# Encoder layer on one core: Squares one row tile ahead, the second w_ada group between the blocks, the fifth pair's weight parts behind the sums

## The chip, the core and the metric

The kernel runs on one NeuronCore of one Trainium2 chip, as one launch. Its engines work side by side: TensorE (PE) multiplies matrices into PSUM banks, VectorE (DVE) and ScalarE (ACT) work elementwise and empty the banks, GpSimd (POOL) sets buffers and issues some stores, and SyncE (SP) issues nearly all transfers. Each engine takes its own instructions strictly in their order and waits on semaphores for the others. The metric is the device time of one execution in microseconds; smaller is better.

## What is computed

The reference is one layer of an encoder on x (1024 rows of 2048), with the parameters of a vector c:

```python
mod = jax.nn.silu(c) @ w_ada + b_ada
shift, scale, gate = jnp.split(mod, 3, axis=-1)
h = rmsnorm(x, pre_g) * (1.0 + scale[:, None]) + shift[:, None]
proj = h @ w_in
...
y_a = windowed_gqa(q, k, v, rel_table, sink) * jax.nn.silu(gate_a)
y_p = multiscale_pool(u, w_pool_grp, pool_scale) * jax.nn.silu(gate_p)
g = jax.nn.sigmoid(h @ w_merge + b_merge)
merged = g_a * (y_a @ w_br_attn) + g_p * (y_p @ w_br_pool)
o = merged @ w_out
return x + gate[:, None] * rmsnorm(o, post_g)
```

All of it is float32. The change touches the first hundred microseconds alone: the norm of x, shift and scale, the making of h, and the first products with w_in.

## The kernel before

**Products.** Every float32 operand is split into a high and a low part (`split`: ACT copies the high part, DVE subtracts it for the low part), and a product is three passes: high by high, high by low, low by high. The large products run by a Strassen scheme (`strassen`): for a pair of 128-column blocks of weights, seven products (X, V and Z are their PSUM banks) with seven moving operands, made from the four quarters of h transposed and named in `MOVING`: B11, T3, T2, B21, T4, T1, B22. "h" and "l" behind a name are the high and low part; whi and wlo are the parts of the weights, raw their loaded tile, ws a sum of two of its quarters.

**The ramp.** x has eight row tiles of 128 rows: 0 to 3 are the left half of h transposed (first index 1 or B11, B21), 4 to 7 the right half (B12, B22). h transposed has 16 tiles k of 128 features; j counts pairs of them. A row tile is normed by `norm_rows` (Squares on ACT and DVE with sums, a DVE reduce of the four sums, then a Sqrt on ACT) and scaled by `scale_rows` on DVE; `turn_part` transposes it on PE (XT) into a PSUM bank, and `take_turned` copies the bank out. A feature tile then needs its scale and shift: `modulation(j)` multiplies silu(c) by 16 tiles of w_ada in four steps (GEMV), ACT copies the sums (acc), PE transposes them (PM), and DVE makes modc of them. Group j = 0 serves k = 0 and 1, group j = 1 k = 2 and 3.

Only then can operands be made. The first four pairs of weight columns (`AHEAD_PAIRS`) take their share of k = 0 and 1 as plain blocks, without the scheme: `plain_blocks(i, s)` is pair i with the left (s = 0) or right (s = 1) half, two PSUM banks of six matmuls (PB), which ACT copies out (c) and POOL's queue stores. `fill_half` makes the operands of these blocks, `fill_sums(0)` those sums of k = 0 and 1 that only the scheme needs, `fill(1)` all operands of k = 2 and 3. With both, pairs five to eight run through the scheme (`ramp_gen`); the first of them, the fifth pair, starts with X at B11.

**What sets the order.** The instructions are put on each engine by a scheduler, but those given to `keep` stay in the order of the program text. The blocks, transposes, GEMVs, Squares, scaling and sums are all kept, so the text from `g0 = modulation(0, ...)` to `fill(1)` sets PE's order, and ACT's and DVE's for the kept ones. `warm(n)` puts n matmuls without a use (WARM) between others. `OPEN` matmuls write the two banks "z0" and "z1" once before Z uses them; they can do so only after ACT has copied the last transposes out of the same banks. `early` and `held` are pools of buffers that end where they are closed.

In the program before, the text is: three steps of group 0 with WARMs, its sums, `fill_half(0)`, `norm_rows(4)`, then for each of four pairs `scale_rows`, `plain_blocks(m, 0)` and the next `norm_rows`; the transposes of k = 0 and 1 with seven WARMs between; `fill_half(1)`; the four pairs' right halves with transposes of k = 2 to 7 between them, and group 1's four steps spread over the last two of them, its PM behind the last block.

Of the kernel before, what the change touches and what calls it, by code (L numbers as in the profile page):

```python
# [43 lines left out]
def encoder_layer(ctx: ExitStack, tc: tile.TileContext, x, c, table, w_ada, b_ada, pre_g,  # L44
# [46 lines left out]
    def keep(ins):  # L91

        tc.keep_in_program_order(ins)

# [9 lines left out]
    @contextmanager  # L104
    def behind(name):

        if name in anchor:
            with tc.issue_after(anchor[name].ins):
                yield
        else:  # L110
            yield
# [110 lines left out]

    def strassen(w, n0, rows, js, op, ev, finish, part=None, raws=None, given=()):

# [45 lines left out]
        def first_weights():  # L270
            yield from given
            if not given:
                yield prep(a11)
                s3 = wp.tile([P, nj, P], F32, tag="ws", name=uid("ws"))
                sub(s3, a11, a21)
                yield prep(s3)
            with behind("blocks" if given else None):
                add(a21, a21, a22)
                sub(a11, a21, a11)
            yield prep(a11)  # L280
# [317 lines left out]
    def fill_sums(j):  # L598

        (b11, b12), (b21, b22) = ((xT[k, 0], xT[k, 1]) for k in (2 * j, 2 * j + 1))  # L600
        keep(sub(b12, b12, b11))
        t2 = rp.tile([P, 512], F32, tag="tf", name=uid("tf"), bufs=2)
        keep(sub(t2, b22, b12))
        keep(sub(b11, t2, b11))
        split(*op["T3"][j], b11, True)
        split(*op["T2"][j], t2, True)
        keep(sub(b21, b21, t2))
        for name, src in (("T4", b21), ("T1", b12)):
            split(*op[name][j], src, True)
# [4 lines left out]
    def ramp_gen(js, i, parts, last):  # L614
        w, n0 = weight_of(RAMP_ORDER[i])
        dst = block(part_d, RAMP_ORDER[i]) if last else block(ramp_d[i], 0)
        return strassen(w, n0, rows_in_turn(0), js, op, ev, to_dram(dst), parts, raws.pop(0))

# [97 lines left out]
    g0 = modulation(0, ada[0].__getitem__, True, True)  # L716
    for step in g0[:2]:
        step()
        warm(3)
    g0[2]()  # L720
    warm(4)
    g0[3]()
    g0[4]()
    warm(3)
    fill_half(0)
    ssq = norm_rows(4)
    for m in range(4):
# [24 lines left out]
    s0, s1, s2, s3, _ = modulation(1, ada[1].__getitem__, True)  # L752
    s0()
    s1()
    plain_blocks(2, 1)
    turn_next((6, 7))
    s2()
    for tag in SEEDED:
        hi = op["B11"][0][0]
        keep(nc.tensor.matmul(bank(tag, "OPEN"), hi[:, 0:P], hi, start=True, stop=True))  # L760
    s3(lambda: plain_blocks(3, 1))
    held.close()
# [924 lines left out]
```

## Time and profile before

| | |
|---|---|
| median of 3 runs | 2110.8 us (2109.87 to 2112.79) |
| the profiled execution | 2110.36 us, its span 2108.6 us |
| mean granted TensorE clock in it | 0.996 |
| PE, DVE, ACT busy | 2074.4, 1549.4, 1112.1 us |

The span is the time from the first to the last instruction of one execution that the hardware profiler recorded; 1.8 us of that execution lie around it. A row of the timeline gives start and duration in us, engine, source line, operation, output<-input by the program's names, shapes and the number of merged instructions; the brackets hold the engine's idle time before it and what ended that. A row of windows gives for a stretch the busy time of each engine with its number of instructions, then the clock that PE was granted (1.00 is full), the DMA engines' busy share (over 1 means more than one transfer at once on an engine) and GB/s.

### The profile page before, as it was taken

How to read it: one execution, taken by the hardware profiler on the slowest of the kernel's cores; microseconds unless marked ns; L12 is line 12 of the kernel's file. 1: busy time of each engine (PE TensorE's matmuls, PEld its weight loads, DVE VectorE, ACT ScalarE, POOL GpSimd, SP SyncE). 2: the span in 40 equal slices, each digit the busy share in tenths (PEclk: the TensorE clock that was granted, in tenths of full speed). 3: DMA queues.
4: the chain of work that ended last, by engine and by line, in shares of the span. 5: the costliest groups of instructions: out<-in, count | busy, mean ns of one | idle time of the engine just before them, and what ended most of it. 6: DMA issues, size and time to landing. Idle time of an engine off the chain costs nothing.

```text
span 2108.6 us, 28906 instructions
## 1 busy us (share of the span) xinstructions
PE 2074.4 (98%) x9473; PEld 1704.8 (81%) x9473; DVE 1549.4 (73%) x2787; ACT 1112.1 (53%) x2114; POOL 42.2 (2%) x135
## 2 busy tenths in 40 slices
PE   6999999999999999999999999999999999999998
PEld 3678788788888888888888888888888788888886
DVE  5696678788547776677777678857957977889667
ACT  5663344444574544665666544333645645767554
POOL 1100000000000000000000000010000000000000
PEclk9999999999999999999999999999999999999999
DMA  9966778999676355454545476675745556686897
GB/s 329 333 216 226 256 246 287 311 320 300 207 242 207 129 176 196 165 166 161 197 153 166 150 241 228 216 239 180 249 156 172 178 195 200 223 308 203 297 332 248
DMA packets 304171, 474.49 MB, mean 225 GB/s; under 512 B 24323, under 2 KB 144235, under 8 KB 304020
## 3 DMA queue, kind: packets, MB, share of 16 engines
q1 hardware_dynamic: 297664, 455.70, 65.3%
q0 software_dynamic: 4896, 14.73, 1.8%
q10 hardware_dynamic: 1460, 2.22, 0.3%
q8 instruction: 74, 1.21, 0.2%
q14 instruction: 77, 0.63, 0.1%
HBM read 344.60 MB, written 130.05 MB: 225 GB/s over the span
## 4 chain that ended last, share of the span: by engine, by line
PE 95%; DVE 2%; DMA 2%; ACT 0%; issue 0%; DVEq 0%; ACTq 0%
PE Z L248 31%; PE X L248 21%; PE V L248 21%; PE Z L1394 2%; PE Z L1396 2%; PE Z L1395 2%; PE X L1395 1%; PE V L1396 1%; PE V L1395 1%; PE X L1396 1%; PE V L1394 1%; PE X L1394 1%; PE PB L691 1%; DMA xt<-in_x_dram 1%; PE PT L1104 1%; PE GEMV L494 1%
## 5 line engine op out<-in xcount | busy, mean ns | idle before, releaser
L96 ACT ACTIVATE whi<-raw 128x512 fp32r<-128x512 f32 (+2 forms) x528 | 319.5, 606 | 527.2 <-PE Z L248 253.3
L97 DVE TENSOR_TENSOR wlo<-raw,whi 128x512 fp32r<-128x512 f32 (+2 forms) x528 | 344.2, 656 | 153.9 <-PE Z L248 121.7
L97 DVE TENSOR_TENSOR wlo<-wr,whi 128x512 fp32r<-128x512 f32 x224 | 150.4, 689 | 51.5 <-ACT whi L96 48.3
L96 ACT ACTIVATE whi<-wr 128x512 fp32r<-128x512 f32 x224 | 138.2, 629 | 87.5 <-DVE wlo L97 30.5
L114 DVE TENSOR_TENSOR raw<-raw,raw 128x512 f32<-128x512 f32 (+1 forms) x80 | 54.7, 683 | 86.0 <-DMA raw<-in_w_merge_dram 57.4
L248 PE MATMUL V<-T3h,whi 128*128 128x512 f32 x332 | 91.1, 393 | 2.3 <-ACT whi L96 1.3
L248 PE MATMUL X<-B11h,whi 128*128 128x512 f32 x332 | 90.8, 391 | 2.3 <-ACT B11h L96 2.3
L248 PE MATMUL Z<-T2h,wlo 128*128 128x512 f32 x332 | 90.2, 391 | 0.8 <-DVE wlo L97 0.8
L96 ACT ACTIVATE whi<-ws 128x512 fp32r<-128x512 f32 (+2 forms) x88 | 53.5, 608 | 71.1 <-PE X L248 62.4
L248 PE MATMUL X<-B11l,whi 128*128 128x512 f32 x332 | 90.2, 390 | 0.8 <-DVE B11l L97 0.8
L114 DVE TENSOR_TENSOR u<-V,u 128x512 f32<-128x512 f32 x94 | 64.6, 687 | 35.6 <-PE V L248 35.0
L248 PE MATMUL X<-B21h,whi 128*128 128x512 f32 x332 | 90.6, 392 | 0.0
L248 PE MATMUL Z<-B22h,whi 128*128 128x512 f32 x332 | 90.6, 392 | 0.0
L248 PE MATMUL Z<-T2h,whi 128*128 128x512 f32 x332 | 90.4, 392 | 0.1
L248 PE MATMUL V<-T3l,whi 128*128 128x512 f32 x332 | 90.4, 391 | 0.0
L248 PE MATMUL Z<-T1h,whi 128*128 128x512 f32 x332 | 90.4, 390 | 0.0
L248 PE MATMUL Z<-T2l,whi 128*128 128x512 f32 x332 | 90.3, 391 | 0.0
L248 PE MATMUL V<-T3h,wlo 128*128 128x512 f32 x332 | 90.1, 391 | 0.0
L248 PE MATMUL V<-T4h,whi 128*128 128x512 f32 x332 | 90.1, 391 | 0.0
L248 PE MATMUL X<-B21l,whi 128*128 128x512 f32 x332 | 89.8, 390 | 0.0
L248 PE MATMUL Z<-B22l,whi 128*128 128x512 f32 x332 | 89.8, 390 | 0.0
L248 PE MATMUL Z<-T1l,whi 128*128 128x512 f32 x332 | 89.8, 389 | 0.0
(366 smaller groups left out, 4882.9 us busy)
## 6 DMA issues: line engine op xcount, KB each, us to landing
part<-part_d SPq DMA_DIRECT2D x136, 256.0 KB, 4.9
ada<-in_w_ada_dram SPq DMA_DIRECT2D x128, 256.0 KB, 6.0
raw<-in_w_merge_dram SPq DMA_DIRECT2D x64, 512.0 KB, 5.7
wr<-ws_dS SPq DMA_DIRECT2D x60, 512.0 KB, 5.3
raw<-in_w_in_dram SPq DMA_DIRECT2D x56, 512.0 KB, 4.0
wr<-in_w_out_dram SPq DMA_DIRECT2D x48, 512.0 KB, 5.3
proj_d<-part SPq DMA_DIRECT2D x68, 256.0 KB, 2.2
sw<-in_w_out_dram SPq DMA_DIRECT2D x64, 256.0 KB, 5.2
```

Of the source, the lines that this page charges most:

```text
L96: ins = (nc.scalar.activation(hi, src, AF.Copy), nc.vector.tensor_tensor(lo, src, f32(hi), ALU.subtract))
L97: nc.vector.tensor_tensor(lo, src, f32(hi), ALU.subtract))
L114: return (eng or nc.vector).tensor_tensor(o, a, b, ALU.add)
L248: nc.tensor.matmul(ps, w_[:, i], op[mov][j][m_], start=fresh and i == 0 and n == 0, stop=i == nj - 1 and n == 2, skip_group_check=True)
L494: ins = nc.tensor.matmul(pv[g:g + 32, :], scz[:, kc, :], tile_of(kc), start=kc < 4, stop=kc >= 12, tile_position=(0, g))
L691: keep(nc.tensor.matmul(open_[nt], w[:, kh, nt * P:(nt + 1) * P], mov[kh][m], start=n == 0, stop=n == 5, skip_group_check=True))
L1104: nc.tensor.transpose(pt[:, i * P:(i + 1) * P], p[:, i * P:(i + 1) * P], ident)
L1394: nc.tensor.matmul(pb, hi, w[0], start=first, stop=False, skip_group_check=True)
L1395: nc.tensor.matmul(pb, lo, w[0], start=False, stop=False, skip_group_check=True)
L1396: nc.tensor.matmul(pb, hi, w[1], start=False, stop=last, skip_group_check=True)
```

## The change

Three things move, and no product is added or dropped.

1. `norm_rows(4)` is issued before the last step of group 0, and inside the loop each `norm_rows` stands ahead of the `scale_rows` of the row tile before it. The WARMs are set anew: five after each of three steps and five after the sums (20 for 13), none between the transposes of k = 0 and 1 (0 for 7), two before the second column's blocks.
2. Group 1's steps are issued after the first right-half pair and its transposes (two steps) and after the second (two steps), with the transposes of k = 4 and 5 between the copy acc and PM. The last two pairs' right halves follow.
3. `strassen` gets `hold`: for the fifth pair, the preparation of its first weight parts (whi, wlo, the sums ws) is issued behind the last split of `fill_sums(0)`, on ACT and on DVE (`anchor["sums", ...]`). Before, `given` and the anchor "blocks" were there without a use.

```diff
-    def behind(name):
+    def behind(name, engine):
-        if name in anchor:
-            with tc.issue_after(anchor[name].ins):
+        if (name, engine) in anchor:
+            with tc.issue_after(anchor[name, engine].ins):
...
         def first_weights():
-            yield from given
-            if not given:
-                yield prep(a11)
-                s3 = wp.tile([P, nj, P], F32, tag="ws", name=uid("ws"))
+            with behind(hold, "v"), behind(hold, "a"):
+                w = prep(a11)
+            yield w
+            s3 = wp.tile([P, nj, P], F32, tag="ws", name=uid("ws"))
+            with behind(hold, "v"), behind(hold, "a"):
                 sub(s3, a11, a21)
-                yield prep(s3)
-            with behind("blocks" if given else None):
+                w = prep(s3)
+            yield w
+            with behind(hold, "v"):
                 add(a21, a21, a22)
                 sub(a11, a21, a11)
...
         for name, src in (("T4", b21), ("T1", b12)):
-            split(*op[name][j], src, True)
+            hi, lo = op[name][j]
+            anchor["sums", "a"] = keep(nc.scalar.activation(hi, src, AF.Copy))
+            anchor["sums", "v"] = keep(sub(lo, src, f32(hi)))
...
-    for step in g0[:2]:
+    for step in g0[:3]:
         step()
-        warm(3)
-    g0[2]()
-    warm(4)
+        warm(5)
+    ssq = norm_rows(4)
     g0[3]()
     g0[4]()
-    warm(3)
+    warm(5)
     fill_half(0)
-    ssq = norm_rows(4)
     for m in range(4):
-        scale_rows(4 + m, ssq)
+        done = ssq
+        ssq = norm_rows(5 + m) if m < 3 else None
+        scale_rows(4 + m, done)
         plain_blocks(m, 0, m == 0)
-        if m < 3:
-            ssq = norm_rows(5 + m)
-    turn_part(1, 0, (0, 1), SEEDED)
-    turn_part(1, 1, (0, 1), SEEDED)
-    turn_part(1, 2, (0, 1), SEEDED)
-    warm(4)
-    turn_part(1, 3, (0, 1), SEEDED)
-    warm(3)
+    for m in range(4):
+        turn_part(1, m, (0, 1), SEEDED)
     fill_half(1)
...
+    s0, s1, s2, s3, _ = modulation(1, ada[1].__getitem__, True)
+    warm(2)
     plain_blocks(0, 1, True)
     turn_next((2, 3))
     fill_sums(0)
-    plain_blocks(1, 1)
-    turn_next((4, 5))
-    s0, s1, s2, s3, _ = modulation(1, ada[1].__getitem__, True)
     s0()
     s1()
+    plain_blocks(1, 1)
+    s2()
+    s3(lambda: turn_next((4, 5)))
     plain_blocks(2, 1)
     turn_next((6, 7))
-    s2()
     for tag in SEEDED:
         hi = op["B11"][0][0]
         keep(nc.tensor.matmul(bank(tag, "OPEN"), hi[:, 0:P], hi, start=True, stop=True))
-    s3(lambda: plain_blocks(3, 1))
+    plain_blocks(3, 1)
...
-        run(ramp_gen((0, 1), i, None, False), side, range(7), at)
+        run(ramp_gen((0, 1), i, None, False, hold=None if n else "sums"), side, range(7), at)
```

What this does to ACT's order at the start. xT are copies of the first transposes, xt_271 and xt_267 parts of row tile 4 (the Squares write over xt_271), ssq its sums, acc group 0's sums. Before:

```order
L449 ACTIVATE xT_152<-XT_146_509 128x512
L501 ACTIVATE acc_586<-GEMV_549 128x512
L549 ACTIVATE B11h_239<-xT_141,modc 128x512
L549 ACTIVATE B21h_251<-xT_143,modc 128x512
L419 ACTIVATE xt_271,ssq_609<-xt_271 128x512
L419 ACTIVATE xt_271,ssq_609<-xt_267 128x512
L426 ACTIVATE ssq_609<-ssq_609,eps_t 128x1
L696 ACTIVATE c_631<-PB_619 128x512
```

And after:

```order
L451 ACTIVATE xT_152<-XT_146_509 128x512
L421 ACTIVATE xt_271,ssq_592<-xt_271 128x512
L421 ACTIVATE xt_271,ssq_592<-xt_267 128x512
L428 ACTIVATE ssq_592<-ssq_592,eps_t 128x1
L503 ACTIVATE acc_603<-GEMV_549 128x512
L551 ACTIVATE B11h_239<-xT_141,modc 128x512
L551 ACTIVATE B21h_251<-xT_143,modc 128x512
L421 ACTIVATE xt_279,ssq_630<-xt_279 128x512
```

Two Squares and the Sqrt of row tile 4 now stand ahead of acc, and the Squares of row tile 5 ahead of the blocks' copies. DVE's two Squares and reduce of row tile 4 move in the same way, ahead of group 0's column sums.

PE around the OPENs, with the transposes of k = 6 and 7 (XT) ahead of them. Before:

```order
L441 MATMUL XT_218_868<-ident,xt_293 128x128
L441 MATMUL XT_219_870<-ident,xt_293 128x128
L494 MATMUL GEMV_839<-ada_315,scz 32x512
L494 MATMUL GEMV_839<-ada_317,scz 32x512
L494 MATMUL GEMV_839<-ada_319,scz 32x512
L494 MATMUL GEMV_839<-ada_321,scz 32x512
L760 MATMUL OPEN_884<-B11h_239 128x512
L760 MATMUL OPEN_886<-B11h_239 128x512
L494 MATMUL GEMV_839<-ada_323,scz 32x512
```

And after:

```order
L443 MATMUL XT_223_891<-ident,xt_293 128x128
L443 MATMUL XT_224_893<-ident,xt_293 128x128
L759 MATMUL OPEN_903<-B11h_239 128x512
L759 MATMUL OPEN_905<-B11h_239 128x512
L695 MATMUL PB_907<-B12h_753,whi_543 128x512
L695 MATMUL PB_907<-B12h_753,wlo_544 128x512
```

The two GEMV steps that stood around the OPENs are now ahead of PM, two pairs of blocks earlier.

PE from the last block to the fifth pair's first products (B11h_239 belongs to k = 0 and 1, B11h_369 to k = 2 and 3). Before:

```order
L691 MATMUL PB_895<-B22l_264,whi_543 128x512
L462 MATMUL PM_914<-ident,acc_892 128x128 x4
L248 MATMUL X_947<-B11h_239,whi_950 128x512
L248 MATMUL V_949<-T3h_243,whi_963 128x512
L248 MATMUL X_947<-B11h_369,whi_950 128x512
L248 MATMUL X_947<-B11l_240,whi_950 128x512
L248 MATMUL X_947<-B11l_370,whi_950 128x512
```

And after:

```order
L695 MATMUL PB_908<-B22l_264,whi_543 128x512
L248 MATMUL X_951<-B11h_239,whi_954 128x512
L248 MATMUL X_951<-B11h_369,whi_954 128x512
L248 MATMUL X_951<-B11l_240,whi_954 128x512
L248 MATMUL X_951<-B11l_370,whi_954 128x512
L248 MATMUL X_951<-B11h_239,wlo_955 128x512
```

PM is gone from this place, and X no longer has a product of V between its own.

More of the change, by code (lines that the diff above doesn't have):

```diff
@@ L91, in keep @@
     def keep(ins):
-        tc.keep_in_program_order(ins)
+        return tc.keep_in_program_order(ins)
     def split(hi, lo, src, pin=False):
@@ L221, in load_parts, with strassen @@
         return parts
-    def strassen(w, n0, rows, js, op, ev, finish, part=None, raws=None, given=()):
+    def strassen(w, n0, rows, js, op, ev, finish, part=None, raws=None, hold=None):
         nj = len(js)
@@ L608, in fill_sums, with ramp_gen @@
         for name, src in (("T4", b21), ("T1", b12)):
-            split(*op[name][j], src, True)
+            hi, lo = op[name][j]
+            anchor["sums", "a"] = keep(nc.scalar.activation(hi, src, AF.Copy))
+            anchor["sums", "v"] = keep(sub(lo, src, f32(hi)))
     RAMP_ORDER = [COL_K, COL_V, COL_GA, COL_GA + 256, COL_Q, COL_GA + 512, COL_GA + 768, COL_Q + 256]
     assert sorted(RAMP_ORDER) == sorted(ORDER[:RAMP])
-    def ramp_gen(js, i, parts, last):
+    def ramp_gen(js, i, parts, last, **kw):
         w, n0 = weight_of(RAMP_ORDER[i])
         dst = block(part_d, RAMP_ORDER[i]) if last else block(ramp_d[i], 0)
-        return strassen(w, n0, rows_in_turn(0), js, op, ev, to_dram(dst), parts, raws.pop(0))
+        return strassen(w, n0, rows_in_turn(0), js, op, ev, to_dram(dst), parts, raws.pop(0), **kw)
     def ramp_raws(i, js):
```

## The prediction

> **What bounds the kernel now.** I read the shares of the page and its chain first, then where TensorE waits (almost all of it in the first 130 us), then the clock in windows, then the timeline of the stretch that the change touches.
>
> ```profile
> PE 2074.4 (98%) x9473; PEld 1704.8 (81%) x9473; DVE 1549.4 (73%) x2787; ACT 1112.1 (53%) x2114; POOL 42.2 (2%) x135
> PE 95%; DVE 2%; DMA 2%; ACT 0%; issue 0%; DVEq 0%; ACTq 0%
> ```
>
> TensorE (PE) is busy for 98% of the span and carries 95% of the chain. So only three things can shorten the run: PE work, PE idle time, or PE running below its clock. The change removes no product, so idle time and clock are left.
>
> ```profile
> 76.67 0.50 PE L248 MATMUL X<-B11h,whi 128*128 128x512 f32 x1 [2.27 <-ACT B11h L96]
> ...
> 78.16 0.50 PE L248 MATMUL X<-B11l,whi 128*128 128x512 f32 x1 [0.76 <-DVE B11l L97]
> ...
> 80.12 0.77 PE L248 MATMUL V<-T3h,whi 128*128 128x512 f32 x1 [0.99 <-ACT T3h L96]
> ```
> ```profile
> 38.20:41.50 3.30, 3.30 (x9) 2.39 (x9) 3.06 (x7) 1.72 (x5) 0.00 (x0) 0.50 1.04 373
> 79.10:85.80 6.70, 5.71 (x14) 4.46 (x14) 5.10 (x11) 3.99 (x9) 0.00 (x0) 0.50 1.10 356
> ```
>
> A timeline row has start, duration, instruction, and in brackets the idle time before it and what ended that. PE stands before the fifth pair's first factors for 2.27 + 0.76 + 0.99 = 4.0 us. In the window rows the three numbers at the end are granted clock, DMA share and GB/s. The clock was 0.50 in two places: 3.4 us around the first block and 6.8 us after those waits. Everything else that I read here ran at 1.00. The whole prize therefore lies between 33 and 90 us.
>
> **The change, part one: Squares of row tile 4 before the factors.** These rows hold the start (PE, then the x loads, then DVE and ACT).
>
> ```profile
> 31.72 2.17 PE L711 MATMUL WARM<-whi 128*128 128x512 f32 x4
> 33.82 1.06 PE L494 MATMUL GEMV<-ada,scz 128*32 128x512 f32 x8
> ...
> 35.68 0.66 PE L462 MATMUL PM<-ident,acc 128*128 128x128 f32 x4 [0.80 <-ACT acc L501]
> ...
> 37.93 0.67 PE L691 MATMUL PB<-B11h,whi 128*128 128x512 f32 x1 [0.57 <-ACT B11h L549]
> ...
> 42.38 0.39 PE L691 MATMUL PB<-B11h,whi 128*128 128x512 f32 x1
> ...
> 50.56 0.81 PE L441 MATMUL XT<-ident,xt 128*128 128x128 f32 x6
> ```
> ```profile
> L412 SPq DMA_DIRECT2D xt<-in_x_dram x4: 327/334/341, 28.5 to 30.7; - x4
> ...
> DMA to landing us min/median/max: 5.6/5.7/5.8
> ```
> ```profile
> 39.82 0.69 DVE L117 TENSOR_TENSOR B21l<-xT,B21h 128x512 fp32r<-128x512 f32 x1
> 40.43 0.68 DVE L421 SCALAR_TENSOR_TENSOR xt<-xt 128x512 f32<-128x512 f32 x1
> ```
> ```profile
> 35.03 0.60 ACT L501 ACTIVATE acc<-GEMV 128x512 f32<-128x512 f32 x1 [8.74 <-PE GEMV L494]
> ...
> 42.15 0.29 ACT L426 ACTIVATE ssq<-ssq,eps_t 128x1 f32<-128x1 f32 x1 [2.20 <-DVE ssq L423]
> 42.35 1.06 ACT L696 ACTIVATE c<-PB 128x512 f32<-128x512 f32 x2
> ```
>
> ACT and DVE stood idle before acc (8.74 us on ACT), so the Squares look free there. They are not. In the new order ACT has two Squares and a Sqrt ahead of acc, and all factors of the first column hang on acc. The last of row tile 4's four loads was issued at 30.7 and took 5.7, so it lands at 36.4. DVE can start then. In the rows Square to Sqrt is 42.15 - 40.43 = 1.72, and the Sqrt occupies ACT for 0.20 (42.35 - 42.15): acc at 36.4 + 1.92 = 38.3 instead of 35.03. The five added WARMs ahead of the last GEMVs cost (33.82 - 31.72) / 4 = 0.53 each, together 2.6. That puts acc at 37.7, so it hides behind the same wait. **Loss 3.3 us.** The bounds are 2.6 (loads no obstacle) and 4 (loads 0.7 later).
>
> From acc the old distances hold: PM after 0.65, first block after 2.90. The five WARMs behind PM replace three and fill the 0.57 of waiting, so PE should not drop to half clock. At full clock the first pair of blocks ends when B21l allows: it ends at 40.51, 2.58 after 37.93, and three matmuls follow. That is about 3.45 instead of 42.38 - 37.93 = 4.45. **Gain 1.0 us.** The other 36 block matmuls took 50.56 - 42.38 = 8.18, which is 0.227 each, and stay.
>
> ```profile
> 52.73 0.78 ACT L549 ACTIVATE B12h<-XT,modc 128x512 fp32r<-128x512 f32 x1 [0.17 <-PE XT L441]
> ```
> ```profile
> 53.56 0.50 PE L691 MATMUL PB<-B12h,whi 128*128 128x512 f32 x1
> ...
> 57.46 1.03 PE L441 MATMUL XT<-ident,xt 128*128 128x128 f32 x8
> ```
>
> Before, the last transposes waited for row tile 7's scaling, and B12h began 2.17 after the blocks' end at 50.56. After, the Squares run one row tile ahead, the scaling is done in time, and B12h follows eight transposes by some 1.0. **Gain 1.15 us.** The seven WARMs taken out stood beside that wait. So the second column's blocks start at 53.56 + 3.3 - 1.0 - 1.15 = 54.7. Up to here the change loses 1.1 us.
>
> **Part two: the second group's sums ahead of three pairs' blocks.** The same GEMVs, blocks and transposes, in another order:
>
> ```profile
> 62.08 1.92 PE L494 MATMUL GEMV<-ada,scz 128*32 128x512 f32 x16
> 63.94 0.51 PE L691 MATMUL PB<-B12h,whi 128*128 128x512 f32 x1
> ...
> 66.83 1.04 PE L441 MATMUL XT<-ident,xt 128*128 128x128 f32 x8
> 67.80 1.07 PE L494 MATMUL GEMV<-ada,scz 128*32 128x512 f32 x8
> 68.79 0.73 PE L760 MATMUL OPEN<-B11h 128*128 128x512 f32 x2
> ...
> 73.33 0.60 PE L462 MATMUL PM<-ident,acc 128*128 128x128 f32 x4
> 73.69 0.48 PE L248 MATMUL X<-B11h,whi 128*128 128x512 f32 x1
> ...
> 89.62 1.06 PE L494 MATMUL GEMV<-ada,scz 128*32 128x512 f32 x8
> ```
> ```profile
> 67.83 1.08 ACT L449 ACTIVATE xT<-XT 128x512 f32<-128x512 f32 x2
> ```
>
> Start to start: 16 GEMVs 1.86, a pair of blocks 2.89, eight transposes 0.97, PM 0.36. Before, from 53.56 to the GEMVs at 89.62 were 36.06 us; of these the first pair's 36 products took 89.62 - 73.69 = 15.93, against 36 x 0.227 = 8.2 without wait and at full clock. Before, PE got B11 76.67 - 73.33 = 3.3 after PM, and T3 6.8 after. In the new order two pairs of blocks and the OPENs stand between PM and the first product: 0.36 + 2.89 + 2.45 + 2.89 = 8.6 (2.45 is worked out below), and T3 is asked for six products later, at 10.0. In between ACT now copies two blocks and two transposed banks ahead of B11, three and two ahead of T3, at 1.08 / 2 each: 2.2 and 2.7 later than before. T3 stands one factor (some 0.6) earlier on ACT than it did. That leaves 8.6 - 3.3 - 2.2 = 3 us of slack for B11 and 10.0 - 6.8 - 2.7 + 0.6 = 1.1 for T3. The weight parts held back until behind the sums are needed later still. So the wait and the half clock go. If they didn't, this part would cost the 0.75 below and bring nothing.
>
> What is late next is OPEN. Two GEMVs stood between the last transposes and OPEN, while ACT emptied the two banks. Now OPEN follows the transposes at once, and ACT's two copies end 2.08 after the blocks (67.83 + 1.08 - 66.83). With one OPEN of 0.37 behind, the next block starts 2.45 after the blocks' end, where 0.97 + 0.73 = 1.70 would do: **loss 0.75**.
>
> New sum from the second column's first block to the same GEMVs: 3.90 (57.46 - 53.56) + 0.97 + 1.86 + 2.89 + 1.86 + 0.97 + 0.36 + 2.89 + 2.45 + 2.89 + 8.2 = 29.2, against 36.06. **Gain 6.8 us**; with 1.1 lost before, **5.7 us**. Behind it the program is unchanged and bound by PE, so I carry 5.7 to the end.
>
> This profiled execution took 2110.4 us with a span of 2108.6, a little below the median of 2110.8. 2110.4 - 5.7 = 2104.7, from the median 2105.1; I say **2104.9**.
>
> **Rivals.** First, the clock. Three windows of 3.41 us, with PE's busy time and count, then clock, DMA share and GB/s:
>
> ```profile
> 34.73:38.14 3.41, 1.99 (x12) 0.99 1.05 386
> 72.20:75.61 3.41, 2.20 (x12) 1.00 1.08 373
> 75.62:79.03 3.41, 1.60 (x5) 1.00 1.08 390
> ```
>
> After the first and third window the clock was at 0.50, after the second it stayed: somewhere between 58% and 65% busy it falls. After the change PE still stands for 1.3 us between the last GEMV and PM. A window that takes in all of it is 62% busy, so the phase decides. A half-clock stretch costs 1.0 here (the old first pair) to 3.41 / 2 = 1.7. **Half clock survives at the start: 5.7 - 1.3 = 4.4, 2106.2.** The Trainium skill ("TensorE: Matmul & The Clock Gate", Part 1) says that the clock halves after a window of some 3.4 us without work, and to keep gaps below about 3 us. By that alone no gap here would matter and the sum above would stand. The trace is stricter: 58% busy was not enough.
>
> Second, transposes may not keep the clock up. Then the stretch of eight transposes, waiting and OPEN (2.45 us) counts as idle, the clock drops in it, and 1.7 us go: 4.0 left, **2106.6**. What the trace has on it, by transposes alone:
>
> ```profile
> 21.27:24.24 2.97, 2.97 (x14) 2.69 (x15) 1.18 (x2) 1.09 (x2) 1.00 1.10 350
> 24.45:25.54 1.09, 1.09 (x11) 1.02 (x10) 0.60 (x1) 0.60 (x1) 1.00 1.10 348
> ```
>
> Fourteen took 2.97, then eleven 1.09: after 3 us of nothing but transposes PE ran twice as fast, so they do count. The skill (same page, Part 4) says the opposite, that transpose mode does not count as busy and leaves the clock low; the trace speaks against it.
>
> Third, **a wait takes the wait's place**: on ACT the copies of blocks stand ahead of B11h and T3h, and my slack there is 1 to 3 us. If some 2.5 us of the old wait come back, 3.2 are left: 2107.4.
>
> Fourth, **data come first**: DMA share is 1.04 to 1.10 in the rows above, so a PE that is early may meet weights that land at a fixed time. The seventh pair's are the nearest.
>
> ```profile
> L198 SPq DMA_DIRECT2D raw<-in_w_in_dram x2: 368/368/368, 74.7 to 75.5; - x2
> ...
> DMA to landing us min/median/max: 7.3/7.3/7.3
> ```
> ```profile
> 103.68 0.61 PE L248 MATMUL X<-B11h,whi 128*128 128x512 f32 x2
> ```
>
> They land at 82.8. Their first product moves from 103.7 to 98, still 15 us later. Gain below 2 if I am wrong: 2109.
>
> Fifth, **slower**: ACT's order makes acc wait for x's row tile 4. Each us that it lands after 36.4 costs one. At 42 the gain is eaten, at 47 the kernel is 0.2% slower, about 2115. The loads before it landed within 0.2 us of each other; nothing in the trace makes them 10 us late.
>
> **Chances.** Forecast (5 to 6.5 gained) 0.56; half clock at the start 0.20; transposes 0.04; new wait 0.12; data 0.04; slower 0.04. A measurement of this kernel tells about 0.2% (4.2 us, 2106.6) from nothing. Faster by more than that holds the forecast nearly whole and two thirds of the clock cases: 0.68. Same 0.29, slower 0.03. The range takes in the clock cases, the new wait, and 1 us of less loss at acc: 2102.8 to 2108.3.
>
> **What would show it.** acc near 38.3 behind Sqrt; the first block near 41.2, and clock 1.00 there; the second column's first block near 54.7; OPEN waiting for ACT's xT by about 0.7; no wait before X, T3h or B11l, clock 1.00 from there on; the first GEMVs of group 2 near 84 instead of 89.62. Acc much later than 38.3, or products of the fifth pair at 0.43 each, would prove me wrong.

## The result and the profile after

| | before | after |
|---|---|---|
| median of 13 runs each, side by side | 2112.15 us (2109.87 to 2113.72) | 2106.56 us (2105.34 to 2108.38) |
| ratio, 95% interval | | 0.9974 [0.9966, 0.9983] |
| profiled execution, its span | 2110.36, 2108.6 us | 2105.86, 2104.1 us |

The change saves 5.6 us by the medians; 5.7 were forecast. The two profiled spans differ by 4.5 only, because this execution of the changed kernel began its first GEMV at 27.19 instead of 25.64, that is ahead of everything the change touches. Distances from row to row are therefore safer than absolute times. PE's timeline of the changed kernel, in rows that answer to those of the prediction:

```profile
27.19 1.07 PE L496 MATMUL GEMV<-ada,scz 128*32 128x512 f32 x8
...
38.12 1.07 PE L496 MATMUL GEMV<-ada,scz 128*32 128x512 f32 x8
39.98 0.66 PE L464 MATMUL PM<-ident,acc 128*128 128x128 f32 x4 [0.79 <-ACT acc L503]
40.39 1.80 PE L715 MATMUL WARM<-whi 128*128 128x512 f32 x5
42.20 0.50 PE L695 MATMUL PB<-B11h,whi 128*128 128x512 f32 x1
...
45.65 0.39 PE L695 MATMUL PB<-B11h,whi 128*128 128x512 f32 x1
...
55.62 0.50 PE L695 MATMUL PB<-B12h,whi 128*128 128x512 f32 x1 [0.29 <-ACT B12h L551]
...
71.33 1.04 PE L443 MATMUL XT<-ident,xt 128*128 128x128 f32 x8
73.02 0.98 PE L759 MATMUL OPEN<-B11h 128*128 128x512 f32 x2 [0.65 <-ACT xT L451]
73.84 0.40 PE L695 MATMUL PB<-B12h,whi 128*128 128x512 f32 x1
...
76.62 0.63 PE L248 MATMUL X<-B11h,whi 128*128 128x512 f32 x2
...
84.89 1.07 PE L496 MATMUL GEMV<-ada,scz 128*32 128x512 f32 x8
```

The first pair of blocks takes 45.65 - 42.20 = 3.45 us. X has no bracket: nothing is waited for. From the second column's first block (55.62) to group 2's GEMVs (84.89) it is 29.27 us, where 36.06 stood before and 29.2 was forecast. From 26.9 us to 2098.8, shortly ahead of the end, the granted clock stays at 1.00; both early stretches at 0.50 are gone.

### The profile page after: what moved, and what is told of

It is laid out like the page before. It is cut to its first block, busy times and chain, and to the rows that moved or that the text cites. A ratio compares the mean times of both kernels' runs of the same rounds, so it can differ in the third digit from the quotient of the medians.

```text
span 2104.1 us, 28920 instructions
## 1 busy us (share of the span) xinstructions
PE 2072.4 (98%) x9475; PEld 1704.0 (81%) x9475; DVE 1550.6 (74%) x2787; ACT 1111.2 (53%) x2114; POOL 42.2 (2%) x135
## 4 chain that ended last, share of the span: by engine, by line
PE 95%; DVE 2%; DMA 2%; ACT 0%; issue 0%; SPq 0%; DVEq 0%; ACTq 0%
PE Z L248 31%; PE V L248 21%; PE X L248 21%; PE Z L1393 2%; PE Z L1394 2%; PE Z L1395 2%; PE V L1394 1%; PE X L1394 1%; PE V L1395 1%; PE X L1395 1%; PE X L1393 1%; PE V L1393 1%; PE PT L1103 1%; PE PB L695 1%; PE GEMV L496 1%; PE PV L1114 0%
## 5 line engine op out<-in xcount | busy, mean ns | idle before, releaser
L114 DVE TENSOR_TENSOR u<-V,u 128x512 f32<-128x512 f32 x94 | 64.7, 689 | 39.0 <-PE V L248 38.3
L248 PE MATMUL V<-T4l,whi 128*128 128x512 f32 x332 | 89.7, 390 | 0.0
L248 PE MATMUL X<-B11h,wlo 128*128 128x512 f32 x332 | 89.7, 390 | 0.0
```

Source lines behind the costliest of these rows:

```text
L114: return (eng or nc.vector).tensor_tensor(o, a, b, ALU.add)
L248: nc.tensor.matmul(ps, w_[:, i], op[mov][j][m_], start=fresh and i == 0 and n == 0, stop=i == nj - 1 and n == 2, skip_group_check=True)
```

## Experiments

After the result two accounts of it were possible. **Theory A** is the prediction's sum: the start loses 1.1 us, the second part gains 6.8, and the two add. **Theory B**: the start, with its full clock, is what gains; **C**: both parts gain; **D** concerns the weight parts alone. When A failed, two more took its place. **E**: two gates stand before the fifth pair's products, group 1's sums and an order on POOL and ACT, and the change opened both. **F**: the second part needs the changed start itself.

All twelve runs in one table. The three columns in the middle come from the profiled execution of each: from the first GEMV to the second column's first block (PB<-B12h), from there to group 2's GEMVs, and both together. The last column is the ratio to the kernel before, run on the same chip.

| run | start | second part | sum, us | median, us | ratio [95%] |
|---|---|---|---|---|---|
| (before) | 27.92 | 36.06 | 63.98 | | 1 |
| (after) | 28.43 | 29.27 | 57.70 | 2106.56 | 0.9974 [0.9966, 0.9983] |
| first_part_only | 30.37 | 34.69 | 65.06 | 2112.59 | 1.0002 [0.9993, 1.0010] |
| second_part_only | 28.33 | 35.42 | 63.75 | 2110.34 | 0.9996 [0.9987, 1.0005] |
| no_hold | 29.17 | 30.36 | 59.53 | 2107.44 | 0.9980 [0.9971, 0.9989] |
| before_warmed | 27.92 | 34.68 | 62.60 | 2111.98 | 1.0001 [0.9992, 1.0010] |
| after_pool_last | 28.56 | 34.65 | 63.21 | 2111.95 | 1.0004 [0.9995, 1.0013] |
| second_fill_first | 28.51 | 32.25 | 60.76 | 2109.98 | 0.9992 [0.9983, 1.0001] |
| both_back_fill | 26.63 | 35.43 | 62.06 | 2110.07 | 0.9990 [0.9981, 0.9999] |
| best_fill | 26.50 | 32.65 | 59.15 | 2107.55 | 0.9981 [0.9973, 0.9990] |
| by_hand_second | 28.35 | 28.85 | 57.20 | 2106.52 | 0.9975 [0.9965, 0.9985] |
| by_hand | 26.64 | 29.33 | 55.97 | 2104.98 | 0.9970 [0.9958, 0.9981] |
| by_hand_open | 26.60 | 29.66 | 56.26 | 2104.81 | 0.9967 [0.9955, 0.9980] |
| after_again | 29.70 | 29.28 | 58.98 | 2106.22 | 0.9975 [0.9965, 0.9985] |

Behind group 2's GEMVs the program is the same, but the profiled executions took between 2018.7 and 2021.7 us from there to their end, so single spans are not compared; the medians and the distances are. Each distance is that of one execution, and how often the clock halved in it differs from one execution to the next: a distance shows where time went, and the median what the run is worth.

### first_part_only

The changed start; the second column in the old order, no `hold`.

```diff
...
+    plain_blocks(1, 1)
+    turn_next((4, 5))
     s0, s1, s2, s3, _ = modulation(1, ada[1].__getitem__, True)
...
-    s3(lambda: turn_next((4, 5)))
...
+    s3(lambda: plain_blocks(3, 1))
...
```

> The start is as after the change, the second column's order is as before it, with no weight parts held back. Theory A: acc near 38.3, first block near 41.2 at full clock, second column's first block 1.1 later than before the change (54.7), then 36 us to the GEMVs of group 2 with the old waits before X, B11l and T3h and the old half clock; time 1.1 us over before (1.0005 of it). Theory B (the start gains): 2 to 5 us under before. Theory C: 1.5 to 3 us under before.

Measured: the same time as before within its interval, and 1.1 us later by the sum column (65.06 against 63.98), as A has it. B and C fall. That A's 1.1 comes out is luck, though, for the sum is made of other pieces: the start is 2.45 longer, the old order of the second part 1.37 shorter (T3h and B11l are no longer waited for, X still 2.27 for B11h). The half clock came back at the first block in this execution, in spite of the five WARMs behind PM; the window ahead of it (PE busy, PEld, DVE, ACT, POOL, then clock):

```profile
37.14:40.55 3.41, 1.76 (x8) 1.14 (x9) 1.15 (x6) 1.21 (x3) 0.00 (x0) 1.00 1.04 372
```

PE was busy for 52% of it, since it stood 1.87 before PM. So the prediction's first rival is real, in one of five profiled executions with this start (the others are the changed kernel twice, no_hold and after_pool_last).

### second_part_only

The old start, the new second part.

```diff
...
-    for step in g0[:3]:
+    for step in g0[:2]:
         step()
-        warm(5)
-    ssq = norm_rows(4)
+        warm(3)
+    g0[2]()
+    warm(4)
...
```

> The start is as before the change; only the order behind the second column's first block (group 1's sums early, OPENs, weight parts queued later) is as after. Theory A (the prediction's sum: the start loses 1.1 us, the second part gains 6.8): acc near 35.0 and the half clock around the first block are back, the second column's first block stands near 53.6, from there to the GEMVs of group 2 it takes 29.2 us (36.06 before), no wait before X, T3h, B11l; time 6.8 us under before, about 1.2 us under the changed kernel. Theory B (the start with its full clock is what gains, the second part only moves a wait): within 1.5 us of before. Theory C (both parts gain): 2 to 4 us under before, and over the changed kernel.

Measured: 0.64 us won in the second part where 6.8 were expected. **Theory A fails here.** PE's waits of old are back, though group 1's sums are early now. First PE, then ACT, then POOL around the fifth pair's first product:

```profile
75.91 0.50 PE L248 MATMUL X<-B11h,whi 128*128 128x512 f32 x1 [1.88 <-ACT B11h L96]
...
78.65 0.76 PE L248 MATMUL V<-T3h,whi 128*128 128x512 f32 x1 [1.00 <-ACT T3h L96]
```
```profile
73.66 0.60 ACT L700 ACTIVATE c<-PB 128x512 f32<-128x512 f32 x1 [0.84 <-PE PB L695]
74.15 0.41 ACT L96 ACTIVATE whi<-raw 128x256 fp32r<-128x256 f32 x1
75.23 0.63 ACT L96 ACTIVATE B11h<-xT 128x512 fp32r<-128x512 f32 x1 [0.67 <-POOL B11l L565]
```
```profile
74.55 0.54 POOL L701 DMA_DIRECT2D ramp_d<-c  x1 [0.90 <-ACT whi L96]
75.08 0.12 POOL L565 MEMSET B11h<- 128x1 f32 x1
```

Before B11h may be written, `claim` (line 565) has POOL set one column of its buffer. Those 14 small MEMSETs are not kept in the text's order. Here they stand on POOL behind the DMA issues of the fourth pair's copies, these wait for ACT's copies c, and the copies wait for the fourth pair's blocks; on ACT the copies themselves stand ahead of B11h too. So B11h cannot come before the last block has ended, whatever happens to the sums. The claims' own share can be read from the bracket: ACT was done with what stands ahead of B11h at 74.56, and B11h waited 0.67 us more for POOL. The changed kernel has the other order on both engines:

```profile
73.33 0.64 ACT L96 ACTIVATE B11h<-xT 128x512 fp32r<-128x512 f32 x1
73.85 0.64 ACT L96 ACTIVATE B21h<-xT 128x512 fp32r<-128x512 f32 x1
...
75.43 0.60 ACT L700 ACTIVATE c<-PB 128x512 f32<-128x512 f32 x1 [0.42 <-PE PB L695]
```
```profile
73.00 0.12 POOL L565 MEMSET B11h<- 128x1 f32 x1
...
76.32 0.54 POOL L701 DMA_DIRECT2D ramp_d<-c  x1 [2.00 <-ACT c L700]
```

(POOL's row names whi as what released it, since that ran then; the copy that it stores ended at 74.26.) The kernel before had both gates: POOL as in the run above, and the sums, whose factors xT end just where B11h starts.

```profile
74.47 0.54 POOL L697 DMA_DIRECT2D ramp_d<-c  x1 [0.90 <-DVE modc L469]
75.00 0.42 POOL L563 MEMSET B11h<- 128x1 f32 x1
```
```profile
74.58 1.52 ACT L549 ACTIVATE xT<-xT,modc 128x512 f32<-128x512 f32 x2
76.00 0.61 ACT L96 ACTIVATE B11h<-xT 128x512 fp32r<-128x512 f32 x1
```

The first part alone has the claims early (70.14 to 71.20 on POOL), but not the sums. Each part opens one gate; alone neither shows much.

### no_hold

```diff
-        run(ramp_gen((0, 1), i, None, False, hold=None if n else "sums"), side, range(7), at)
+        run(ramp_gen((0, 1), i, None, False, hold=None), side, range(7), at)
```

> The changed kernel with the fifth pair's weight parts no longer held back until the sums are done; TensorE's order is the same. Theory A (the parts are needed late, holding them back is worth nothing): the GEMVs of group 2 at the same distance (29.2 us) from the second column's first block, within 0.5 us; time within 0.5 us of the changed kernel, 5 to 6 us under before. Theory D (without the hold, VectorE makes two weight differences ahead of T3l and T2l, and TensorE waits for these): a wait of 0.5 to 1.5 us before V<-T3l or Z<-T2l, a half-clock window of some 1.7 us may follow; 1 to 3 us over the changed kernel.

Measured: 2107.44 us, not to be told from the changed kernel by the times, but 1.09 us more in the second part: A's 0.5 is missed, and D's wait is not there either. Instead VectorE's two weight differences, of which the first stands 2.35 us for its loads, delay the sum behind T4h, ACT's queue moves with it, and acc stands in a full queue, so that PM waits (DVE, then ACT, then PE):

```profile
61.91 0.43 DVE L117 TENSOR_TENSOR ws<-raw 128x256 f32<-128x256 f32 x1 [2.35 <-DMA raw<-in_w_in_dram]
```
```profile
64.99 0.63 ACT L612 ACTIVATE T4h<-xT 128x512 fp32r<-128x512 f32 x1 [2.67 <-DVE xT L117]
...
67.31 0.60 ACT L503 ACTIVATE acc<-GEMV 128x512 f32<-128x512 f32 x1
```
```profile
67.96 0.66 PE L464 MATMUL PM<-ident,acc 128*128 128x128 f32 x4 [0.87 <-ACT acc L503]
```

In the changed kernel T4h waited 1.45, and PM nothing (68.10, straight behind the transposes).

### before_warmed

The kernel before with five WARMs behind group 1's PM.

```diff
     s3(lambda: plain_blocks(3, 1))
+    warm(5)
```

> The kernel before, with five WARM matmuls behind the sums' transposes PM, where TensorE stands waiting for the fifth pair's first factors: about 2.65 us of filler in 3.3 us of wait. It parts the 7.6 us that the second part takes from the fifth pair's products into waiting (4.0) and half clock (3.6 to 3.7). Theory A: the clock stays at 1.00 between 79 and 86 us, the wait before X<-B11h shrinks to nothing while its products start at the same time (76.7), B11l and T3h are still waited for; the GEMVs of group 2 come 3 to 3.7 us earlier than 89.6; time 3 to 3.7 us under before. Rival (the half clock hides further waits: at full clock the products meet factors that come at a fixed time): less than 1.5 us under before, and waits of over 1 us before T3h, T3l or T4.

Measured: no gain in time, 1.38 us by the second part's column; the rival is nearer. The wait before X shrinks from 2.27 to 1.23 and others stay, and the clock still falls for one window:

```profile
78.19 0.50 PE L248 MATMUL X<-B11h,whi 128*128 128x512 f32 x1 [1.23 <-ACT B11h L96]
...
81.12 1.22 PE L248 MATMUL Z<-T2h,whi 128*128 128x512 f32 x2 [0.67 <-ACT Z L286]
```
```profile
81.00:84.30 3.30, 3.18 (x8) 2.53 (x9) 3.30 (x7) 1.72 (x5) 0.00 (x0) 0.50 1.10 360
```

So filler does not part the 7.6 us into waiting and half clock, and that split was not settled. This run shows something else, too. Its first pair of blocks ran at full clock, and the second column still came 15.62 us after the first block, where the kernel before with its half clock has 15.63:

```profile
53.58 0.44 PE L441 MATMUL XT<-ident,xt 128*128 128x128 f32 x2 [0.99 <-DVE xt L432]
```

With the old order of scaling the last transposes wait for row tile 7 in any case, and a half clock in the first pair of blocks costs nothing there.

### after_pool_last

The changed kernel with the claims of the second factors behind the fourth pair's DMA issues again; the scheduler then also put the copies ahead of B11h.

```diff
...
+            anchor["put", "p"] = nc.gpsimd.dma_start(block(ramp_d[i], 0)(f"{nt + 1}{s + 1}"), t)
...
     plain_blocks(3, 1)
+    with behind("put", "p"):
+        for name in MOVING:
+            for t in op[name][1]:
+                nc.gpsimd.memset(f32(t)[:, 0:1], 0.0)
```

> The changed kernel with one thing put back: POOL's 14 small memsets that claim the buffers of the second factors (B11h, B11l, T3h ... B22l; 75.0 us in the kernel before, 73.0 in the changed one) stand again behind the DMA issues of the fourth pair's block copies, and with them the scheduler puts these copies ahead of B11h on ScalarE, as in the run of the second part alone. Theory E (two gates stand before the fifth pair's products, group 1's sums and these claims; the change opened both, the second one through the order that the scheduler chose): B11h starts about 1.5 us behind the fourth pair's last block, X<-B11h is waited for by 1.9 to 2.3 us, the clock falls to 0.50 for one or two windows; the time is 4 to 5 us over the changed kernel, within 1.5 us of before. Theory F (the start of the changed kernel, not the claims, is what the second part lacked): time as the changed kernel, 5 to 6 us under before, no wait before X.

Measured: 1.0004 of before; the whole gain is gone, and 5.4 us are back in the second part. E as expected, F falls. X, V and the clock lose as in the run of the second part alone (1.87 and 1.00 us of waiting, 0.50 from 81.5 to 84.9). The edit also moves the last two claims, of B22h and B22l, to 82.54 and 83.09, where the kernel before has them by 76.1; no wait of PE ends on them.

```profile
77.99 0.63 ACT L96 ACTIVATE B11h<-xT 128x512 fp32r<-128x512 f32 x1 [0.67 <-POOL B11l L765]
```
```profile
78.67 0.50 PE L248 MATMUL X<-B11h,whi 128*128 128x512 f32 x1 [1.87 <-ACT B11h L96]
```

### second_fill_first

The second part alone; the fourth pair's copies behind B11h on ACT, their DMA issues behind the claims on POOL.

```diff
...
-    plain_blocks(3, 1)
+    puts = []
+    plain_blocks(3, 1, puts=puts)
     held.close()
     fill(1)
+    with behind("B11h", "a"), behind("claim", "p"):
+        for p in puts:
+            p()
```

> The second part alone (start as before the change), and the claims on POOL and B11h on ScalarE put ahead of the fourth pair's copies by hand. Theory E: nothing is waited for before X, T3h, B11l, the clock stays at 1.00 there, from the second column's first block to the GEMVs of group 2 it takes 29.2 us; the half clock around the first block is still there; 6 to 7 us under before (5.5 under the second part alone). Theory F: as the second part alone, 1.5 us under before, the wait before X stays.

Measured: 3.8 us of the second part, not 6.9, and by the medians 1.9 us under before where E had 6 to 7. The clock stayed at 1.00, at the first block too, but the waits stayed as well. The claims ended at 73.3, yet B11h came only 1.3 us earlier after the second column's first block than in second_part_only (21.04 for 22.34; 17.71 in the changed kernel), for a third instruction now stood ahead of it:

```profile
75.78 0.42 ACT L96 ACTIVATE whi<-raw 128x256 fp32r<-128x256 f32 x1 [3.37 <-PE PB L696]
76.10 0.61 ACT L96 ACTIVATE B11h<-xT 128x512 fp32r<-128x512 f32 x1
```

A weight part of the fifth pair waited for the fourth pair's blocks, by its place the last readers of its buffer. The copies, in turn, came so late (79.49) that V waited 1.4 us for them. E's numbers are missed here, and the run does not decide between E and F, since the order that E needs was not reached.

### both_back_fill

As the last one, but with the changed kernel's start less two things: three WARMs behind each step for five, and row tile 4's Squares behind the first factors. Squares one row tile ahead and five WARMs behind PM stay.

```diff
...
-        warm(5)
-    ssq = norm_rows(4)
+        warm(3)
     g0[3]()
     g0[4]()
     warm(5)
     fill_half(0)
+    ssq = norm_rows(4)
...
```

> As the last one, and of the start three things more: row tile 4's Squares stay behind the first factors and the WARMs between the GEMVs are as before (3, 3, 3), so acc hangs on the GEMVs alone; the Squares run one row tile ahead, and five WARMs stand behind PM, as in the change. Prediction's terms: the loss of 3.3 at acc goes, the 1.15 at the end of the first column stays won: 1.15 us under the run before it; if five WARMs behind PM keep the clock at 1.00 in the first pair's blocks (3.45 instead of 4.45 us), 2.15 under it, 8 to 9 us under before. Rival: one WARM fewer ahead of the GEMVs of the last step lets the clock fall anyway, 7 to 8 us under before.

Measured: the start is 1.88 us shorter than in the run before it, where 1.15 to 2.15 were expected: 1.26 behind the first block and 0.62 ahead of it, where one WARM is gone. The first pair is at full clock (3.44 us), but so it was in the run before it, so the 1.0 for the clock was not there to be won. The fifth pair's products wait as there, and in this execution the clock fell for two windows (78.2 to 85.1), so the second part costs 35.43, and the median is 1.8 us under before where 8 to 9 were expected.

### best_fill

As the last one, OPEN behind the fourth pair's blocks.

```diff
...
-    for tag in SEEDED:
-        hi = op["B11"][0][0]
-        keep(nc.tensor.matmul(bank(tag, "OPEN"), hi[:, 0:P], hi, start=True, stop=True))
     puts = []
     plain_blocks(3, 1, puts=puts)
+    for tag in SEEDED:
+        hi = op["B11"][0][0]
+        keep(nc.tensor.matmul(bank(tag, "OPEN"), hi[:, 0:P], hi, start=True, stop=True))
...
```

> As the last one, with the two OPEN matmuls behind the fourth pair's blocks instead of ahead of them, so that they do not wait for ScalarE's copies of the transposed banks. Prediction's term: 0.75 us less (the wait of 0.65 before OPEN goes, nothing is late instead), 9 to 9.6 us under before. Rival: the blocks of the fourth pair now use the time and the products stand waiting for B11l or the banks by as much: no difference to the last one.

Measured: 2107.55, 4.4 us under before (9 to 9.6 expected), with one window at half clock where the last run had two; so the difference of 2.78 us in the second part is not OPEN's alone: one such window is worth up to 1.7. The question was put again below.

### by_hand_second

The second part alone, with ACT's, DVE's and POOL's order around the fifth pair's factors written as the changed kernel has it.

```diff
...
+        hi("T2", t2)
+        lo("T2", t2)
+        with behind("claim", "p"):
+            puts[0]()
+        keep(sub(b21, b21, t2))
+        hi("T1", b12)
+        hi("T3", b11)
+        with behind("claim", "p"):
+            puts[1]()
...
-        product(prep(a12), "B21", bx)
+        with behind("fill" if hold else None, "a"):
+            w = prep(a12)
+        product(w, "B21", bx)
...
```

> The start as before the change, and the second part with ScalarE's, VectorE's and POOL's order around the fifth pair's factors written out by hand, so that it is the order of the changed kernel (claims ahead of the fourth pair's DMA issues; B11h, B21h, T2h, copy, T1h, T3h, copy, B22h, T4h; the fifth pair's fourth weight part behind T4h). Theory E (the second part needs this order and nothing of the start): no wait before X, T3h or B11l, clock 1.00 from the second column on, 29.2 us from the second column's first block to the GEMVs of group 2 (32.3 in the run before it, 35.4 in the second part alone, 36.06 before); 6 to 7 us under before. Theory F (it needs the changed start too): a wait of 1 us or more somewhere among the fifth pair's products, 2 to 3 us under before at most.

Measured: 28.85 us in the second part, nothing waited for, clock 1.00 from 25.2 to 2100.5; 0.9975 of before, which is 4.9 us by the medians and 3.2 to 7.4 by the interval (6 to 7 expected). E holds: with the order right the second part has the gain by itself, and nothing of the changed start is needed. Between these two executions it is 7.2 us, 6.8 with the two WARMs at its head (0.43 in the start column). The 7.2 counts the half clock of the one execution of the kernel before; the medians are the safer number.

```profile
70.98 0.12 POOL L567 MEMSET B11h<- 128x1 f32 x1
```
```profile
71.31 0.64 ACT L592 ACTIVATE B11h<-xT 128x512 fp32r<-128x512 f32 x1
```
```profile
54.06 0.40 PE L727 MATMUL PB<-B12h,whi 128*128 128x512 f32 x1
...
74.61 0.63 PE L248 MATMUL X<-B11h,whi 128*128 128x512 f32 x2
...
82.91 1.06 PE L498 MATMUL GEMV<-ada,scz 128*32 128x512 f32 x8
```

### by_hand

The same with the start of both_back_fill; its edit is the sum of those two.

> The same order by hand, and the start in which row tile 4's Squares stay behind the first factors, WARMs between the GEMVs as before (3, 3, 3), five WARMs behind PM, Squares one row tile ahead. Theory E with the prediction's terms for the start: from the first GEMV to the second column's first block 26.6 us (27.9 before, 28.4 in the changed kernel), the first pair at full clock, then 29.2; 7.5 to 8.5 us under before, 2 to 3 under the changed kernel. Rival (what is won early is given back where a transfer lands at a fixed time): as the changed kernel, 5 to 6 under before, with a wait for a transfer behind 85 us.

Measured: 26.64 and 29.33, both as expected, and no wait for a transfer. The median is 2104.98 us, 6.5 under before and 1.2 under the changed kernel on the same chip (7.5 to 8.5 and 2 to 3 expected). By the sum column it is 1.7 to 3.0 us ahead of the two executions of the changed kernel, but the intervals of the ratios (up to 0.9981, and from 0.9965) overlap, so the times do not show that it beats it.

### by_hand_open

As the last one, OPEN behind the fourth pair's blocks.

> As the last one, with the two OPEN matmuls behind the fourth pair's blocks. Prediction's term: the wait of 0.65 before OPEN goes; 0.75 us less than the last one, 28.5 us from the second column's first block to the GEMVs of group 2. Rival (T3l is late next: it ended only 0.66 ahead of its product in the changed kernel): 0.3 us less at most, and a wait of some tenths before V<-T3l.

Measured: nothing won (29.66 against 29.33). The wait before OPEN is gone, the products begin 0.97 us earlier after the second column's start (72.59 - 52.54 = 20.05, by_hand 21.02), and then wait for T3:

```profile
74.62 0.47 PE L248 MATMUL V<-T3h,whi 128*128 128x512 f32 x1 [0.27 <-ACT T3h L592]
...
75.76 0.47 PE L248 MATMUL V<-T3l,whi 128*128 128x512 f32 x1 [0.44 <-DVE T3l L117]
```

The rival holds: T3l is next in line, and in this order of ACT and DVE the 0.75 us of OPEN is not to be had.

### after_again

The changed kernel, unedited.

> The changed kernel once more, on the chip of these three, to compare with: 5 to 6 us under before (forecast 5.7; 5.5 measured). The part of the forecast that is the start: 28.4 to 29.2 us from the first GEMV to the second column's first block.

Measured: 0.9975 as the first time, 29.28 in the second part. The start is 29.70, a little over what was expected, and shows acc behind the Sqrt, with no wait in between:

```profile
35.79 0.63 ACT L421 ACTIVATE xt<-xt 128x512 f32<-128x512 f32 x1 [10.15 <-DMA xt<-in_x_dram]
...
38.21 0.29 ACT L428 ACTIVATE ssq<-ssq,eps_t 128x1 f32<-128x1 f32 x1 [0.94 <-DVE ssq L425]
38.41 0.58 ACT L503 ACTIVATE acc<-GEMV 128x512 f32<-128x512 f32 x1
```

## Why the prediction was right, and where its reason was not

- **acc at 38.3.** Right in place and size: 38.12, 38.22 and 38.41 where the GEMVs began by 25.3 (first_part_only, no_hold, after_again), each 0.20 behind the start of the Sqrt. In the profiled execution of the change they began at 27.19, and the WARMs' own delay, which I had hidden behind the x loads, was the longer one: acc at 39.33, 12.14 after the first GEMV instead of 9.39, so 2.75 lost (after_pool_last is alike: 26.60, acc at 38.85). The losses measured, 2.75 to 4.0 (13.43 in after_again), are about the bounds I gave, 2.6 to 4.
- **+1.0 for the first pair and +1.15 behind it.** The sum came out: 13.42 us from first block to second column instead of 15.63, 2.21 for 2.15. Its parts were wrong. before_warmed had the first pair at full clock and gained nothing, since row tile 7 was waited for all the same; and with the old start and the second part it is 16.04 us both at half clock (second_part_only) and at full (second_fill_first). The gain comes from the Squares one row tile ahead, together with the WARMs gone from between the transposes, which no run parts from it; only then does a half clock cost anything, 0.77 (14.19 in first_part_only). With row tile 4's Squares back behind the first factors the distance is 14.77 (by_hand): ACT's copy of the first pair's blocks then stands behind two row tiles' Squares, and PE waits 0.60 for it.
- **Loss of 1.1 up to the second column.** By the start column 0.5 and 1.8 in the two executions of the changed kernel, 1.25 in no_hold and 0.6 in after_pool_last, which share its start: 1.05 in the mean, with 2.45 in first_part_only left out, where the half clock came. The earlier the first GEMV, the larger the loss, since row tile 4 is then waited for.
- **6.8 from the second part.** The size was right (6.79 and 6.78), the reason incomplete, and this is the step that failed. I wrote that the wait and the half clock go because the sums come earlier and leave 3 us of slack for B11 and 1.1 for T3. With the sums early and nothing else, 0.64 us were gained. I had read the slack from the changed program's order on ACT, and there it came out (B11h ended at 73.97, 2.65 ahead of X; T3h at 77.08, 0.92 ahead of V). But I did not ask what holds B11h back on POOL, nor whether that order belongs to this part of the change. It does not: it came along only when both parts were there, and after_pool_last takes away the whole gain by it. by_hand_second shows that the order is enough, given the early sums. That the scheduler put the claims and B11h early in the changed kernel was no part of my reasoning, so the number is in part luck. Which of the three instructions ahead of B11h (claims, copies, weight part) holds it by itself was not parted (in second_part_only the claims are the last, by 0.67 us), and why the scheduler chooses so differently after the two starts stays open.
- **OPEN, 0.75 lost.** Measured 73.84 - 71.33 = 2.51 for the forecast 2.45. But with the order of by_hand it is no loss that can be taken back.
- **Weight parts held back, at nothing.** By the second part's column of one execution the hold is worth 1.1 us, through acc and PM, because without it DVE stands for weight loads ahead of the last sums; by the times it is too small to tell.
- **The rivals.** Half clock at the start came in one execution of five and cost 0.77 where I had put 1.0 to 1.7. The transposes did not bring it: in the changed kernel the 2.51 us of transposes, wait and OPEN passed at 1.00. The window of the clock that holds them has 2.77 us of PE work, 1.04 of it the transposes; without these it would have 1.73, and in the ramp every window with less than 2.0 halved the clock (last section). (The prediction's two rows on transposes both read 1.00 because the record of the clock begins only at 24.44 in that execution, with a rise to 1.00; the speed of the transposes doubles there.) A new wait did not come in the changed kernel, but in second_part_only it did, and for the reason given: copies ahead of B11h on ACT, with the claims besides. Data first and slower did not come.

```profile
71.26:74.68 3.42, 2.77 (x16) 1.98 (x14) 1.47 (x4) 3.19 (x8) 2.27 (x16) 1.00 1.07 369
```

## What to carry to other kernels

When an early result does not bring an early start, look at what stands ahead of the consumer on its own queue, and at the cheap instructions on other engines that must come first: a buffer's claim behind a DMA issue can hold the chain behind it, here by 0.67 us. Before summing the parts of a change, ask for each whether the order that it relies on is its own or comes from another part; where a scheduler decides it, write the order down. Then a part brings its gain by itself.

## What the runs showed of the hardware

In the ramp the clock's limit is narrow. It changed only in steps of 3.41 us, counted in each execution from the first rise in its record of the clock (23.34 in second_part_only, 24.03 in after_again, 26.96 in second_fill_first). These windows lie on the steps; columns as above. The first halved the clock, the second and third did not:

```profile
33.58:36.99 3.41, 1.99 (x12) 1.02 (x9) 0.67 (x4) 1.61 (x3) 0.00 (x0) 1.00 1.05 386
36.99:40.40 3.41, 3.41 (x9) 2.52 (x10) 3.17 (x7) 1.84 (x5) 0.00 (x0) 0.50 1.07 381
```
```profile
37.68:41.10 3.42, 2.02 (x9) 1.25 (x9) 0.90 (x6) 1.47 (x3) 0.00 (x0) 1.00 1.04 341
...
41.10:44.51 3.41, 3.37 (x13) 2.05 (x13) 3.02 (x7) 2.16 (x6) 0.00 (x0) 1.00 1.05 378
```
```profile
78.16:81.57 3.41, 2.03 (x9) 1.11 (x7) 3.41 (x7) 3.25 (x8) 1.07 (x2) 1.00 1.11 349
81.57:84.98 3.41, 3.41 (x17) 2.77 (x16) 2.70 (x7) 2.87 (x7) 0.00 (x0) 1.00 1.09 366
```

They are from second_part_only, after_again and second_fill_first: 1.99 us of PE work in 3.41 was too little, 2.02 and 2.03 were enough, in executions whose matmul ends are modelled. Counted like this over the first 2090 us of all fourteen profiled executions, the ten windows that halved the clock hold 1.36 to 1.99 us of PE work, and every window that kept it at 1.00 at least 2.02. At 0.50, windows with 2.42 to 2.72 us left the clock there, and 3.31 or more raised it. The steps lie differently in each execution, so a wait of 1.87 halved the clock in one (first_part_only) and one of 2.0 did not in another (after_again). The Trainium skill ("TensorE: Matmul & The Clock Gate", Part 1) names an idle window of some 3.4 us as what halves the clock; the width of the step agrees, but here no window was idle, and 58% of work was not enough.

Busy time by the profile is not itself what the clock goes by, though. Where the products end, close to the end of by_hand, 1.68 us in a window kept the clock, and only the empty window behind it halved it:

```profile
2091.91:2095.32 3.41, 1.68 (x8) 1.06 (x6) 1.54 (x4) 0.98 (x3) 0.00 (x0) 1.00 0.71 249
2095.32:2098.73 3.41, 0.00 (x0) 0.00 (x0) 2.56 (x4) 0.00 (x0) 0.00 (x0) 1.00 0.60 213
```

In both_back_fill 1.81 us were enough at that place. The work in these two windows is products without a gap, in the ramp it is short groups with waits between; what the clock does count stays open.
